# A diagonal state-space loop: chunks read back through a buffer in memory, table products added in PSUM, input factors cut from the state matrices

## The chip, the cores and the metric

The kernel runs on one core of a Trainium2 chip. The metric is the device time of one execution in microseconds (us). Engines are named as the profile names them: PE (matrix products), DVE (vector), ACT (scalar), POOL and SP; each executes its own instructions strictly in the order in which they were written for it, DMA issues included.

## The reference, cut to what matters

A two-layer decoder trunk on 256 tokens of width 1024: attention, a dense feed-forward layer ("ffn"), the state-space layer ("s5") and a layer of eight experts ("moe"). The change is in the state-space layer:

```python
u = (h @ w_in).reshape(B, S, 64, 16)                 # 64 groups of 16 channels
bbr = gr * br - gi * bi;  bbi = gr * bi + gi * br    # input factors, (64, 64 states, 16)
bu_r = einsum('bsgh,gph->sbgp', u, bbr); bu_i = einsum('bsgh,gph->sbgp', u, bbi)
xr, xi = scan over s of  x[s] = a * x[s-1] + bu[s]   # a complex and diagonal, per group and state
y = einsum(xr, c_re) - einsum(xi, c_im) + d_skip * u
z = gelu(y) @ w_glu
out = z[..., :D] * sigmoid(z[..., D:])
```

## The kernel before, in words

The four layers run one after the other, and weights stream from memory on SP's DMA queue through a ring of buffers. In all layers but the experts a weight of 128x1024 is split into a high and a low part, `whi` on ACT (L227) and `wlo` on DVE (L229), three pairs of buffers deep, and each product is made of three matmuls (L253 to L255).

In `s5` the 256 tokens are cut into 32 chunks of 8, and the 64 groups into 8 blocks `b` of 8 groups. First `pu`, the product with `w_in`, is made in two halves of 512 columns; ACT scales each into `ut` (L1040). Then, per block:

- T, `tables` (L865): DVE makes `cp`, the output factors times the powers of `a` (L874), as two products and a sum (L876), and `bt`, the input factors, as two products and a sum (L879, L880). SP loads `bc` and `dd`.
- A, `local` (L885): PE multiplies `bt` by `cp` into `pkk`; ACT copies it to `kk` (L898), DVE adds the skip term (L899), and eight DMAs, four on SP and four on POOL, spread it into the 128x128 blocks of `tt` (L902), which POOL has cleared.
- X, `chunks` (L912): eight DMAs of 32x128 from `ut`, issued on ACT's queue, gather the block's tokens by chunk into `X` (L916).
- U, `chunkT` (L918): PE transposes `X` into `pU`, ACT copies it to `U` (L924).
- S, `states` (L926): PE multiplies `U` by the state matrices `M` into `pS` (L931); DVE rotates (`ri`), scans (`z`), rotates back (`ro`) and writes `W` (L942).
- P, `output` (L945): PE adds `tt`·`U` (L951) and `cp`·`W` (L954) in `py`.
- Z, `gelu` (L957): DVE transposes `py` into `yd`, ACT takes the gelu and the high part `gTh`, DVE the low part `gTl`.
- G and H, `glu`: twelve matmuls into `pz` with one split weight. `pq` is a part of the same product with other columns, for all eight blocks.

The order in which blocks and steps are written is a list, `ORDER`; a scheduler then fixes each engine's own order. Below a block is named by its number: S3 is the state product of block 3. The layer's last loop product is P7. The matrices `M` are made earlier, during the ffn layer, by `s5_tables`: there DVE multiplies the same input matrices by the factors for 8 powers into `mt`, PE transposes them.

Of the kernel before, what the change touches and what calls it, by code (L numbers as in the profile page):

```python
# [10 lines left out]
F32 = mybir.dt.float32  # L11
# [3 lines left out]
AF = mybir.ActivationFunctionType  # L15
ALU = mybir.AluOpType
# [3 lines left out]
P = 128  # L20
D = 1024
KB = D // P
TOK = 256
TB = TOK // P
# [7 lines left out]
CH = 8  # L32
NCK = TOK // CH
# [39 lines left out]
PROL = "0:T0 1:T1 2:A0"  # L73
AQ = "spspspsp"
KBUF = 3
MANUAL = 0
RING, RING2, LOOK = 4, 2, 2
LOOK2 = 3
# [24 lines left out]
class Trunk:  # L103
# [637 lines left out]
    def s5_tables(self, m, t):  # L741
        nc, a, v = self.nc, self.a, self.nc.vector
        G = 64
# [3 lines left out]
        n = lambda nm: t.tile([P, G], F32, tag="z_" + nm, name="z_" + nm)  # L747
# [23 lines left out]
        while k < 8:  # L771
            b = lambda z: z[:, k:k + 1, :].to_broadcast([P, k, G])
# [7 lines left out]
        g = t.tile([P, 2, G], F32, name="gri")  # L780
# [14 lines left out]
            v.tensor_mul(g[:, i, :], u1, den)  # L795
        H = (t.tile([P, 8, G], F32, name="Hr"), t.tile([P, 8, G], F32, name="Hi"))
        gb = [g[:, i:i + 1, :].to_broadcast([P, 8, G]) for i in range(2)]
        self.Bt = m.tile([P, 2, G], F32, name="Bt")
        v.tensor_copy(self.Bt, g)
        yield  # L800
        self.cmul(t, H, (pr[:, 0:8], pi[:, 0:8]), gb, [P, 8, G], "Hc")
        for z in (pr, pi):
# [8 lines left out]
        for i in range(7):  # L811
            q = (t.tile([P, G], F32, tag="rc", name="rc", bufs=2), t.tile([P, G], F32, tag="rs", name="rs", bufs=2))
            self.cmul(t, q, r[-1], r[-1], [P, G], "rq")
            r.append(q)
            if i >= 2:
# [4 lines left out]
                else:  # L820
                    h = max(1, k // 2)
# [8 lines left out]
        for b in range(8):  # L830
            gs = slice(b * 8, b * 8 + 8)
            B = t.tile([P, 2, 8, 16], F32, tag="Bb", name="Bb", bufs=2)
            nc.sync.dma_start(B, a["s5bc"][b][:, 2:4])
            mt = [t.tile([P, 8, 8, 16], F32, tag=f"mt{i}", name=f"mt{i}") for i in range(2)]
            for i in range(2):
                v.tensor_tensor(mt[i], B[:, i, :, None, :].to_broadcast([P, 8, 8, 16]),
                                H[i][:, :, gs].rearrange("p j g -> p g j")[:, :, :, None].to_broadcast([P, 8, 8, 16]), op=ALU.mult)
            v.tensor_tensor(mt[0], mt[0], mt[1], op=ALU.add)
            for q in range(2):
                pt = self.tp((P, 4, P), name="MT")  # L840
                for i in range(4):
                    nc.tensor.transpose(pt[:, i, :], mt[0][:, q * 4 + i].rearrange("p j h -> p (j h)"), self.ident)
                g0 = b % 2 * 8 + q * 4
                nc.scalar.copy(self.M[b // 2][:, g0:g0 + 4, :], pt)
            yield

    def s5(self, h, m, t):
        nc, a, v = self.nc, self.a, self.nc.vector
        mm = nc.tensor.matmul
# [2 lines left out]
        with self.behind((None, self.h_dve, self.t_dve)[H1 // 8 % 4]):  # L852
            self.upto("moe")
        r2 = self.rms(h, "n2", self.t_act if H1 & 32 else None)
        ut = t.tile([P, TB, D], F32, name="ut")
        gh, gl = self.xT("gT")
        CP, T, M8, BT, U, W, Y, XS, DD = {}, {}, {}, {}, {}, {}, {}, {}, {}

        flip = [0]

        def alt(shape, name):
            flip[0] ^= 1
            return (self.gu, self.tp)[flip[0]](shape, name)

        def tables(b):  # L865
            gs = slice(b * 8, b * 8 + 8)
            bc = t.tile([P, 4, 8, 16], F32, tag="bc", name="bc", bufs=2)
            nc.sync.dma_start(bc, a["s5bc"][b])
            DD[b] = t.tile([16, 8, 16], F32, tag="dd", name="dd", bufs=2)
            nc.sync.dma_start(DD[b], a["s5_dd"][:, gs])  # L870
            cp = t.tile([P, 8, 9, 16], F32, tag="cp", name="cp", bufs=KBUF)
            ct = t.tile([P, 8, 9, 16], F32, tag="t16", name="ct", bufs=2)
# [11 lines left out]
            CP[b], M8[b], BT[b] = cp, m8, bt[0]  # L884

        def local(b):
            cp, bt = CP[b], BT.pop(b)
            kk = t.tile([16, 8, P], F32, tag="t16", name="kk", bufs=2)
            tt = T[b] = t.tile([P, 8, P], F32, tag="tt", name="tt", bufs=KBUF)
            nc.gpsimd.memset(tt, 0.0)  # L890
            pk = alt((P, 2, P), name="pkk")
            for q in range(2):
                for i in range(4):
                    g = 2 * i + q
                    mm(pk[32 * i:32 * i + 16, q, :], lhsT=bt[:, g, :], rhs=cp[:, g, 0:8, :].rearrange("p d h -> p (d h)"),
                       start=True, stop=True)
# [14 lines left out]

        def chunks(b):  # L912
            X = XS[b] = self.tmp.tile([NCK, CH, 16, 8], F32, tag="xn", name="X")
            for j in range(CH):
                tb, jj = divmod(j, CH // TB)
                nc.scalar.dma_start(X[:, CH - 1 - j].rearrange("c h g -> c (h g)"), ut[jj * NCK:(jj + 1) * NCK, tb, b * P:(b + 1) * P])  # L916

        def chunkT(b):  # L918
            X = XS.pop(b)
# [25 lines left out]
        def output(b):  # L945
            u, w, cp, tt = U[b], W[b], CP[b], T[b]
            py = Y[b] = alt((P, 2, P), name="py")
            for q in range(2):
                for i in range(4):
                    g = 2 * i + q  # L950
                    mm(py[32 * i:32 * i + 32, q, :], lhsT=u[:, g, :], rhs=tt[:, g, :], start=True, stop=False)  # L951
                for i in range(4):
                    g = 2 * i + q
                    mm(py[32 * i:32 * i + 32, q, :], lhsT=w[:, g, :], rhs=cp[:, g, 1:9, :].rearrange("p d h -> p (d h)"),  # L954
                       start=False, stop=True)

        def gelu(b):  # L957
            py = Y.pop(b)
# [21 lines left out]
        def glu_out(nh):  # L980
            for tb in range(TB):
# [35 lines left out]
        def run(w, k):  # L1017
            if 0 <= k < 8 and (w, k) not in done:
                done.add((w, k))
                steps[w](k)  # L1020
                for e, tag in pf:
                    if e == f"{w}{k}":
                        self.early(tag)

        for n in range(2):
            pu = [self.acc("pu") for _ in range(TB)]
            for u in range(2):
                for hf in range(2):
# [12 lines left out]
            if n == 0:  # L1041
                run("X", 0)
        for i in range(-4, 16):
# [406 lines left out]
def trunk_kernel(ctx: ExitStack, tc: tile.TileContext, a, out, stage=9):  # L1450
    nc = tc.nc
    if MANUAL:
        ctx.enter_context(tc.manual_schedule())
    t = Trunk(ctx, tc, a, out)
    h = t.mla()
    if stage == 1:
        nc.sync.dma_start(out.rearrange("(b p) d -> p b d", p=P), h)
# [117 lines left out]
```

## Time and profile before

| | us |
|---|---|
| median of 3 runs (1354.12 to 1358.92) | 1354.19 |
| the profiled execution | 1351.04 |
| its span, first to last instruction | 1348.9 |
| PE busy in the span | 1271.1 (94%) |
| DVE busy | 500.5 (37%) |
| ACT busy | 315.1 (23%) |
| read from memory | 417.19 MB |

The profiled execution lasted 2.1 us longer than its span. Shares over the whole span hide the layers: attention and ffn fill the first 327 us, `s5` the stretch from there to about 485, the experts the rest. The page's table of 40 slices shows where an engine is busy; a slice is 33.7 us long.

### The profile page before, as it was taken

Reading aid. Unit: us, or ns where it says so; the run is one execution under the profiler, and the core shown is the slowest. Engines: PE = TensorE matmul, PEld = TensorE weight load, DVE = VectorE, ACT = ScalarE, POOL = GpSimd, SP = SyncE. Lnnn points to the kernel's source line nnn. Section 1 sums busy time; section 2 is a strip of 40 time slices with the busy share of each in tenths; the row PEclk is TensorE's granted clock in tenths of the full one; section 3 lists DMA queues with packets and bytes.
Section 4 is the critical chain, followed back from the end, with each engine's and each line's share of the span. In section 5 each row is a group of like instructions: output and inputs, shape, how many; then the busy total and the mean of one; then the engine's idle time right before and its main releaser. Section 6 shows DMA issues by size and latency. Waiting matters only on the chain. (4 is left out here: it accounts for less than half of the span.)

```text
span 1348.9 us, 38996 instructions
## 1 busy us (share of the span) xinstructions
PE 1271.1 (94%) x17345; PEld 882.9 (65%) x17345; DVE 500.5 (37%) x1085; ACT 315.1 (23%) x630; POOL 48.5 (4%) x89
## 2 busy tenths in 40 slices
PE   7898999999888899999999999999999999999973
PEld 6787999997676776666656665555655555665542
DVE  5875989887778750102020011002002002011102
ACT  6764544455323450100010000001000001000001
POOL 3000000001023100000000000000000000000000
PEclk9989999999877899999999999999999999999997
DMA  7303445553444779999999999999999999999993
GB/s 286 125 33 104 178 178 181 195 199 141 159 133 123 258 291 407 416 414 415 416 416 416 418 407 405 417 407 407 415 419 405 405 405 417 413 404 415 408 402 130
DMA packets 80448, 424.26 MB, mean 315 GB/s; under 512 B 14608, under 2 KB 18448, under 8 KB 39824
## 3 DMA queue, kind: packets, MB, share of 16 engines
q1 hardware_dynamic: 76016, 418.79, 78.3%
q0 software_dynamic: 1024, 1.31, 0.7%
q8 instruction: 138, 2.26, 0.7%
q10 hardware_dynamic: 3232, 1.58, 0.5%
q14 instruction: 38, 0.31, 0.1%
HBM read 417.19 MB, written 1.05 MB: 310 GB/s over the span
## 5 line engine op out<-in xcount | busy, mean ns | idle before, releaser
L1235 PE MATMUL pg<-w,xg 128*32 128x256 f32 (+1 forms) x7168 | 492.5, 378 | 5.6 <-DMA w<-in_moe_w 5.5
L1235 PEld LDWEIGHTS pg<-w,xg 128*32 128x32 f32 x7168 | 262.6, 110 | 160.8 <-issue 11.9
L1325 PE MATMUL py<-w,th 128*32 128x256 f32 x4704 | 280.3, 380 | 6.2 <-DMA w<-in_moe_w 6.1
L1271 DVE TENSOR_TENSOR sl<-pg,sl 128x256 f32<-128x256 f32 (+1 forms) x56 | 23.6, 422 | 672.4 <-ACT sl L1270 672.4
L1325 PEld LDWEIGHTS py<-w,th 128*32 128x32 f32 x4704 | 160.4, 110 | 107.0 <-DMA w<-in_moe_w 6.8
L1235 PE MATMUL pu<-w,xg 128*32 128x256 f32 (+1 forms) x2240 | 226.9, 376 | 1.5 <-issue 1.5
L1270 ACT ACTIVATE sl<-pg 128x256 f32<-128x256 f32 (+1 forms) x56 | 21.4, 381 | 653.1 <-PE pg L1235 653.1
L229 DVE TENSOR_TENSOR wlo<-w,whi 128x1024 fp32r<-128x1024 f32 (+1 forms) x120 | 141.3, 1182 | 47.9 <-ACT whi L227 47.6
L227 ACT CAST whi<-w 128x1024 fp32r<-128x1024 f32 (+1 forms) x120 | 121.6, 1019 | 130.2 <-PE pg L254 52.1
L1235 PEld LDWEIGHTS pu<-w,xg 128*32 128x32 f32 x2240 | 100.8, 110 | 48.5 <-issue 2.8
L254 PE MATMUL pg<-n1l,whi 128*128 128x256 f32 x352 | 101.7, 289 | 0.0
L253 PE MATMUL pg<-n1h,whi 128*128 128x256 f32 x352 | 101.4, 288 | 0.1
L255 PE MATMUL pg<-n1h,wlo 128*128 128x256 f32 x352 | 101.5, 289 | 0.0
L253 PEld LDWEIGHTS pg<-n1h,whi 128*128 128x128 f32 x352 | 67.5, 192 | 1.3 <-ACT whi L227 0.3
L254 PEld LDWEIGHTS pg<-n1l,whi 128*128 128x128 f32 x352 | 67.6, 192 | 0.7
L255 PEld LDWEIGHTS pg<-n1h,wlo 128*128 128x128 f32 x352 | 67.4, 192 | 0.0
L253 PE MATMUL fo<-whi,th 128*128 128x512 f32 x88 | 34.6, 394 | 0.3 <-ACT th L700 0.3
L254 PE MATMUL fo<-wlo,th 128*128 128x512 f32 x88 | 34.5, 393 | 0.0
L255 PE MATMUL fo<-whi,tl 128*128 128x512 f32 x88 | 34.3, 390 | 0.0
L1404 POOL TENSOR_TENSOR fx<-h,gF 128x512 f32<-128x512 f32 x1 | 1.3, 1274 | 883.8 <-ACT fjk L1403 883.8
L1273 DVE STREAM_TRANSPOSE th<-sl 128x384 f32<-128x384 f32 (+2 forms) x56 | 29.4, 525 | 2.0
L1369 PE MATMUL psc<-yy,ST 96*128 96x512 f32 (+1 forms) x64 | 24.9, 465 | 5.2 <-ACT yy L1362 2.7
(469 smaller groups left out, 1383.9 us busy)
## 6 DMA issues: line engine op xcount, KB each, us to landing
w<-in_moe_w SPq DMA_DIRECT2D x264, 1024.0 KB, 16.9
w<-in_moe_w SPq DMA_DIRECT2D x144, 512.0 KB, 13.6
w<-in_ffn_gu SPq DMA_DIRECT2D x22, 1024.0 KB, 4.8
w<-in_ffn_dn SPq DMA_DIRECT2D x11, 1024.0 KB, 4.8
w<-in_s_glu SPq DMA_DIRECT2D x8, 1024.0 KB, 6.0
w<-in_mla_o SPq DMA_DIRECT2D x4, 1024.0 KB, 4.8
w<-in_s_in SPq DMA_DIRECT2D x4, 1024.0 KB, 4.7
w<-in_mla_in SPq DMA_DIRECT2D x4, 672.0 KB, 7.4
```

What stands on the lines that cost most here:

```text
L227: nc.scalar.copy(hi[:, :k], w[:, c0:c1])
L229: self.lo_dve = nc.vector.tensor_sub(lo[:, :k], w[:, c0:c1], hi[:, :k].bitcast(F32))
L253: mm(out, lhsT=lh, rhs=rh, start=first, stop=False)
L254: mm(out, lhsT=lh, rhs=rl, start=False, stop=False)
L255: mm(out, lhsT=ll, rhs=rh, start=False, stop=last)
L1235: mm(ps[t // 2][32 * q:32 * q + 32, t % 2, 0:w], lhsT=lhsT, rhs=rhs[:, q], start=first and t % 2 == 0, stop=last and (t % 2 == 1 or t == n ...
L1270: self.silu = nc.scalar.activation(sl[:, ts], src[:, :, 0:k], AF.Silu)
L1271: v.tensor_tensor(sl[:, ts], src[:, :, k:2 * k], sl[:, ts], op=ALU.mult)
L1273: v.transpose(th.rearrange("p t b x -> p (t b x)"), sl.rearrange("p t k -> p (t k)"))
L1325: mm(y[e][b][32 * q:32 * q + 32, i, :], lhsT=th[:, t, fb], rhs=w[:, c * 256:(c + 1) * 256], start=first and i == 0, stop=last and (nt == 2 ...
L1369: mm(ps, lhsT=gath[e][0:CAPS[e], tb * P:(tb + 1) * P], rhs=yy[:, z], start=z == 0, stop=z == 1)
L1404: (nc.gpsimd, v)[n if XM else 1].tensor_mul(x[:, 1, s], h[:, 1, s], gF[:, s])
```

## The change

- X is one DMA on SP instead of eight on ACT. `ut` is now a buffer of one half, written by two DMAs on ACT's queue to a buffer in memory (`du0`, `du1`), and `X` is read back from there with the chunks reversed by the access pattern.
- The sum of the two products of `cp` is gone: both stay as tiles, and PE multiplies by each and adds in PSUM, in `pkk` and in `py`.
- `bt` is gone: the factors for power 0 are copied by ACT from `mt` to `BT` in the ffn layer, and `bc` loads half as much.
- `kk` has one buffer of its own (it shared two with a product of `cp`), `tt` two buffers instead of three, and `ut` takes turns with `X` in the two buffers `xn`.

```diff
 def s5_tables
-        self.Bt = m.tile([P, 2, G], F32, name="Bt")
-        v.tensor_copy(self.Bt, g)
+        self.BT = m.tile([P, G, 16], F32, name="BT")
...
             v.tensor_tensor(mt[0], mt[0], mt[1], op=ALU.add)
+            nc.scalar.copy(self.BT[:, gs, :], mt[0][:, :, 0, :])
 def s5
-        ut = t.tile([P, TB, D], F32, name="ut")
+        UT = [self.dram.tile([TB, P, 512], F32, name=f"du{n}") for n in range(2)]
 def tables
-            bc = t.tile([P, 4, 8, 16], F32, tag="bc", name="bc", bufs=2)
+            bc = t.tile([P, 2, 8, 16], F32, tag="bc", name="bc", bufs=2)
...
-            for i, (o, z) in enumerate(((cp, self.pr), (ct, self.pi))):
-                v.tensor_tensor(o, bc[:, i, :, None, :].to_broadcast([P, 8, 9, 16]),
+            for i, z in enumerate((self.pr, self.pi)):
+                v.tensor_tensor(CP[b][i], bc[:, i, :, None, :].to_broadcast([P, 8, 9, 16]),
...
-            v.tensor_tensor(cp, cp, ct, op=ALU.add)
-            bt = [t.tile([P, 8, 16], F32, tag=f"bt{i}", name=f"bt{i}") for i in range(2)]
-            for i in range(2):
-                v.tensor_tensor(bt[i], bc[:, 2 + i], self.Bt[:, i, gs, None].to_broadcast([P, 8, 16]), op=ALU.mult)
-            v.tensor_tensor(bt[0], bt[0], bt[1], op=ALU.add)
 def local
-            kk = t.tile([16, 8, P], F32, tag="t16", name="kk", bufs=2)
-            tt = T[b] = t.tile([P, 8, P], F32, tag="tt", name="tt", bufs=KBUF)
+            kk = t.tile([16, 8, P], F32, tag="kk", name="kk", bufs=1)
+            tt = T[b] = t.tile([P, 8, P], F32, tag="tt", name="tt", bufs=2)
...
-                    mm(pk[32 * i:32 * i + 16, q, :], lhsT=bt[:, g, :], rhs=cp[:, g, 0:8, :]...,
-                       start=True, stop=True)
+                for n in range(2):
...
+                        mm(pk[32 * i:32 * i + 16, q, :], lhsT=self.BT[:, b * 8 + g, :], rhs=cp[n][:, g, 0:8, :]...,
+                           start=n == 0, stop=n == 1)
 def chunks
-            for j in range(CH):
-                tb, jj = divmod(j, CH // TB)
-                nc.scalar.dma_start(X[:, CH - 1 - j]..., ut[jj * NCK:(jj + 1) * NCK, tb, b * P:(b + 1) * P])
+            n, i = divmod(b, 4)
+            row = UT[n][:, :, :]
+            src = bass.AP(tensor=row.tensor, offset=row.offset + i * P, ap=[[512, NCK], [NCK * 512, CH], [1, P]])
+            nc.sync.dma_start(X.rearrange("c j h g -> c j (h g)")[:, ::-1], src)
 def output
-                    mm(py[32 * i:32 * i + 32, q, :], lhsT=w[:, g, :], rhs=cp[:, g, 1:9, :]..., start=False, stop=True)
+                for n in range(2):
...
+                        mm(py[32 * i:32 * i + 32, q, :], lhsT=w[:, g, :], rhs=cp[n][:, g, 1:9, :]..., start=False, stop=n == 1)
 in s5, after each half of pu
+            ut = self.tmp.tile([P, TB, 512], F32, tag="xn", name="ut")
             for tb in range(TB):
-                nc.scalar.activation(ut[:, tb, n * 512:(n + 1) * 512], pu[tb], AF.Copy, scale=r2[:, tb:tb + 1])
+                nc.scalar.activation(ut[:, tb], pu[tb], AF.Copy, scale=r2[:, tb:tb + 1])
+                nc.scalar.dma_start(UT[n][tb], ut[:, tb])
```

ACT's order from the end of the first half of `pu` on, before:

```order
L1040 ACTIVATE ut<-pu,n2y 128x512
L916 DMA X<-ut 32x128
L1040 ACTIVATE ut<-pu,n2y 128x512
L916 DMA X<-ut 32x128 x7
L227 CAST whi<-w 128x1024 x2
L898 COPY kk<-pkk 16x256 x4
L227 CAST whi<-w 128x1024
L924 COPY U<-pU 128x256
L916 DMA X<-ut 32x128
```

and now (the product of `local` for block 0 has moved ahead of it, into the first half of `pu`):

```order
L1039 ACTIVATE ut<-pu,n2y 128x512
L1040 DMA du_3871<-ut 128x512
L1039 ACTIVATE ut<-pu,n2y 128x512
L228 CAST whi<-w 128x1024
L1040 DMA du_3871<-ut 128x512
L228 CAST whi<-w 128x1024 x3
L1039 ACTIVATE ut<-pu,n2y 128x512
L1040 DMA du_3872<-ut 128x512
L1039 ACTIVATE ut<-pu,n2y 128x512
L921 COPY U<-pU 128x256
L1040 DMA du_3872<-ut 128x512
```

Seven gathers stood between `ut` and the next `whi`; now no more than one write stands between any two. SP's order at the blocks 0 to 2, now (before, the same queue without its `X` rows):

```order
L898 DMA tt<-kk 16x8x16
L898 DMA tt<-kk 16x8x48
L898 DMA tt<-kk 16x8x80
L898 DMA tt<-kk 16x8x112
L913 DMA X<-du_3871 32x8x128
L871 DMA dd<-in_s_dd 16x128
L869 DMA bc<-in_s5bc 128x256
L206 DMA w<-in_s_glu 128x2048
L913 DMA X<-du_3871 32x8x128
L206 DMA w<-in_s_glu 128x2048
L898 DMA tt<-kk 16x8x16
```

The reads stand among the copies of `tt` and the weights, each behind what precedes it. DVE's order around `W` of block 2, before:

```order
L229 TENSOR_TENSOR wlo<-w,whi 128x1024
L937 SCALAR_TENSOR_TENSOR z<-m8b,ri_4315 128x256
L964 TENSOR_TENSOR gTl<-yd,gTh 128x256
L907 TENSOR_TENSOR ro_4323<-z,E 128x256
L908 TENSOR_TENSOR ro_4324<-z,F 64x256
L909 TENSOR_TENSOR ro_4324<-z,F 64x256
L907 TENSOR_TENSOR ri_4446<-pS,E 128x256
L942 TENSOR_TENSOR W<-ro_4323,ro_4324 128x8x31
```

and now:

```order
L874 TENSOR_TENSOR cp<-bc,pi 128x1152
L934 SCALAR_TENSOR_TENSOR z<-m8b,ri_4319 128x256
L230 TENSOR_TENSOR wlo<-w,whi 128x1024
L903 TENSOR_TENSOR ro_4327<-z,E 128x256
L904 TENSOR_TENSOR ro_4328<-z,F 64x256
L905 TENSOR_TENSOR ro_4328<-z,F 64x256
L230 TENSOR_TENSOR wlo<-w,whi 128x1024
L939 TENSOR_TENSOR W<-ro_4327,ro_4328 128x8x31
```

The split of the weight after next has moved ahead of `W`.

## Rows read from the trace of the kernel before

**Rows 1.** The page's 40 slices: busy tenths of PE and the clock granted to it, in tenths.
```profile
PE   7898999999888899999999999999999999999973
PEclk9989999999877899999999999999999999999997
```

**Rows 2.** Busy time by stretch (us from the span's start, its length; then PE, PEld, DVE, ACT, POOL with their instructions, the granted clock, DMA share, GB/s): the loop of the eight blocks, what follows it up to the experts, the experts.
```profile
347.00:457.00 110.00, 89.56 (x724) 72.23 (x722) 80.51 (x145) 35.76 (x71) 27.09 (x55) 0.75 0.47 127
457.00:500.00 43.00, 42.51 (x225) 33.04 (x217) 30.46 (x80) 26.78 (x48) 0.00 (x0) 1.00 0.82 327
600.00:1330.00 730.00, 715.32 (x12417) 422.02 (x12408) 89.92 (x192) 51.65 (x137) 0.00 (x0) 1.00 1.00 407
```

**Rows 3.** Waits of PE in the loop, 347 to 457 us: who waited for whom, us in total, times, the longest.
```profile
PE pS L931 <- ACT U L924: 7.5, 5, 2.9
PE pz L253 <- ACT gTh L963: 3.9, 1, 3.9
PE pU L922 <- DMA dd<-in_s_dd: 3.3, 2, 2.1
PE pU L922 <- DMA X<-ut: 2.0, 2, 1.7
PE pkk L895 <- ACT kk L898: 1.6, 1, 1.6
```

**Rows 4.** Groups of ACT in the same stretch: count, busy us, mean ns of one, idle just before them and what ended it.
```profile
L227 ACT CAST whi<-w 128x1024 fp32r<-128x1024 f32 x12 | 12.5, 1046 | 31.7 <-PE pz L255 18.7 <-DMA X<-ut 9.5 <-PE pu L255 3.2
L898 ACT COPY kk<-pkk 16x256 f32<-16x256 f32 x32 | 11.6, 363 | 10.0 <-DMA dd<-in_s_dd 5.6 <-DMA X<-ut 4.1
L924 ACT COPY U<-pU 128x256 f32<-128x256 f32 x8 | 3.0, 370 | 10.4 <-DMA X<-ut 8.3 <-PE pU L922 1.7 <-PE py L951 0.4
L962 ACT ACTIVATE yd<-yd 128x256 f32<-128x256 f32 x7 | 2.9, 417 | 12.8 <-DVE yd L960 12.8
L963 ACT CAST gTh<-yd 128x256 fp32r<-128x256 f32 x7 | 2.8, 406 | 0.3
...
L962 ACT ACT_TABLE_LOAD x1 | 1.3, 1283 | 7.2 <-DMA X<-ut 7.2
```

**Rows 5.** The gathers by source line: issues on ACT's queue, ns of one issue (min, median, max), first and last start.
```profile
L916 ACTq DMA_DIRECT2D X<-ut x64: 513/601/1882, 347.8 to 416.7; - x64
```

**Rows 6.** ACT in order of time (start, us, instruction, idle before it and who ended it), at the second half of `pu`.
```profile
347.08 0.69 ACT L1040 ACTIVATE ut<-pu,n2y 128x512 f32<-128x512 f32 x1 [0.94 <-PE pu L255]
...
348.49 6.31 ACTq L916 DMA_DIRECT2D X<-ut  x7
354.84 1.99 ACT L227 CAST whi<-w 128x1024 fp32r<-128x1024 f32 x2 [5.68 <-DMA X<-ut]
```

**Rows 7.** PE in order of time, same columns: the stop in the second half of `pu`; S0; a `pkk` group at the high and one at the low clock; S2; the first and last of a block's twelve `pz` matmuls at the low clock and at the high; the last `py` group of P7.
```profile
352.77 0.39 PE L255 MATMUL pu<-whi,n2l 128*128 128x512 f32 x1
...
355.94 1.22 PE L253 MATMUL pu<-whi,n2h 128*128 128x512 f32 x2 [2.22 <-ACT whi L227]
...
365.36 1.87 PE L931 MATMUL pS<-U,M 128*128 128x32 f32 x16
367.16 0.63 PE L895 MATMUL pkk<-cp,bt 128*16 128x128 f32 x16
...
376.63 1.08 PE L895 MATMUL pkk<-cp,bt 128*16 128x128 f32 x16
...
380.51 3.62 PE L931 MATMUL pS<-U,M 128*128 128x32 f32 x16 [1.42 <-ACT U L924]
...
408.74 0.80 PE L253 MATMUL pz<-whi,gTh 128*128 128x512 f32 x1
...
413.60 0.53 PE L255 MATMUL pz<-whi,gTl 128*128 128x512 f32 x1
...
453.24 0.39 PE L253 MATMUL pz<-whi,gTh 128*128 128x512 f32 x1
...
455.75 0.39 PE L255 MATMUL pz<-whi,gTl 128*128 128x512 f32 x1
...
456.75 0.40 PE L954 MATMUL py<-cp,W 128*32 128x128 f32 x8
```

**Rows 8.** DVE: in order of time, the `W` that answers to S0; then groups of the loop, 347 to 457 us (count, busy us, mean ns, idle before).
```profile
371.86 0.40 DVE L942 TENSOR_TENSOR W<-ro,ro 128x248 f32<-128x248 f32 x1
...
L229 DVE TENSOR_TENSOR wlo<-w,whi 128x1024 fp32r<-128x1024 f32 x12 | 14.5, 1212 | 8.8 <-ACT whi L227 8.8
L876 DVE TENSOR_TENSOR cp<-cp,ct 128x1152 f32<-128x1152 f32 x7 | 9.4, 1348 | 0.0
L879 DVE TENSOR_TENSOR bt<-bc,Bt 128x128 f32<-128x128 f32 x13 | 3.6, 281 | 0.0
...
L960 DVE STREAM_TRANSPOSE yd<-py 128x256 f32<-128x256 f32 x7 | 3.1, 441 | 2.3 <-PE py L954 2.3
```

**Rows 9.** DMA issues by line in 347 to 457 and at the kernel's end (KB each, median us from issue to landing): a load, and the kernel's output, which goes to memory; then the smallest, median and largest landing of the gathers and of the output.
```profile
bc<-in_s5bc SPq DMA_DIRECT2D x8, 256.0 KB, 3.3
out<-fx ACTq DMA_DIRECT2D x2, 256.0 KB, 5.7
...
DMA to landing us min/median/max: 1.7/2.7/6.6
...
DMA to landing us min/median/max: 3.1/4.8/6.7
```

More of the change, by code (lines that the diff above doesn't have):

```diff
@@ L75 @@
 KBUF = 3
+KQ = "sss"
 MANUAL = 0
@@ L854, in s5 @@
         r2 = self.rms(h, "n2", self.t_act if H1 & 32 else None)
-        ut = t.tile([P, TB, D], F32, name="ut")
+        UT = [self.dram.tile([TB, P, 512], F32, name=f"du{n}") for n in range(2)]
         gh, gl = self.xT("gT")
-        CP, T, M8, BT, U, W, Y, XS, DD = {}, {}, {}, {}, {}, {}, {}, {}, {}
+        CP, T, M8, U, W, Y, XS, DD = {}, {}, {}, {}, {}, {}, {}, {}
         flip = [0]
@@ L866, in tables @@
             gs = slice(b * 8, b * 8 + 8)
-            bc = t.tile([P, 4, 8, 16], F32, tag="bc", name="bc", bufs=2)
-            nc.sync.dma_start(bc, a["s5bc"][b])
+            bc = t.tile([P, 2, 8, 16], F32, tag="bc", name="bc", bufs=2)
+            nc.sync.dma_start(bc, a["s5bc"][b][:, 0:2])
             DD[b] = t.tile([16, 8, 16], F32, tag="dd", name="dd", bufs=2)
             nc.sync.dma_start(DD[b], a["s5_dd"][:, gs])
-            cp = t.tile([P, 8, 9, 16], F32, tag="cp", name="cp", bufs=KBUF)
-            ct = t.tile([P, 8, 9, 16], F32, tag="t16", name="ct", bufs=2)
-            for i, (o, z) in enumerate(((cp, self.pr), (ct, self.pi))):
-                v.tensor_tensor(o, bc[:, i, :, None, :].to_broadcast([P, 8, 9, 16]),
+            CP[b] = [t.tile([P, 8, 9, 16], F32, tag=f"cp{i}", name="cp", bufs=KBUF) for i in range(2)]
+            for i, z in enumerate((self.pr, self.pi)):
+                v.tensor_tensor(CP[b][i], bc[:, i, :, None, :].to_broadcast([P, 8, 9, 16]),
                                 z[:, :, gs].rearrange("p j g -> p g j")[:, :, :, None].to_broadcast([P, 8, 9, 16]), op=ALU.mult)
-            v.tensor_tensor(cp, cp, ct, op=ALU.add)
-            bt = [t.tile([P, 8, 16], F32, tag=f"bt{i}", name=f"bt{i}") for i in range(2)]
-            for i in range(2):
-                v.tensor_tensor(bt[i], bc[:, 2 + i], self.Bt[:, i, gs, None].to_broadcast([P, 8, 16]), op=ALU.mult)
-            v.tensor_tensor(bt[0], bt[0], bt[1], op=ALU.add)
             m8 = t.tile([P, 8, NCK], F32, tag="m8b", name="m8b", bufs=2)
@@ L883, in tables @@
             nc.gpsimd.memset(m8[:, :, 0:1], 0.0)
-            CP[b], M8[b], BT[b] = cp, m8, bt[0]
+            M8[b] = m8
         def local(b):
-            cp, bt = CP[b], BT.pop(b)
-            kk = t.tile([16, 8, P], F32, tag="t16", name="kk", bufs=2)
-            tt = T[b] = t.tile([P, 8, P], F32, tag="tt", name="tt", bufs=KBUF)
+            cp = CP[b]
+            kk = t.tile([16, 8, P], F32, tag="kk", name="kk", bufs=1)
+            tt = T[b] = t.tile([P, 8, P], F32, tag="tt", name="tt", bufs=2)
             nc.gpsimd.memset(tt, 0.0)
@@ L892, in local @@
             for q in range(2):
-                for i in range(4):
-                    g = 2 * i + q
-                    mm(pk[32 * i:32 * i + 16, q, :], lhsT=bt[:, g, :], rhs=cp[:, g, 0:8, :].rearrange("p d h -> p (d h)"),
-                       start=True, stop=True)
+                for n in range(2):
+                    for i in range(4):
+                        g = 2 * i + q
+                        mm(pk[32 * i:32 * i + 16, q, :], lhsT=self.BT[:, b * 8 + g, :], rhs=cp[n][:, g, 0:8, :].rearrange("p d h -> p (d h)"),
+                           start=n == 0, stop=n == 1)
             for i in range(4):
@@ L951, in output @@
                     mm(py[32 * i:32 * i + 32, q, :], lhsT=u[:, g, :], rhs=tt[:, g, :], start=True, stop=False)
[L952 to L955, printed above, removed]
+                for n in range(2):
+                    for i in range(4):
+                        g = 2 * i + q
+                        mm(py[32 * i:32 * i + 32, q, :], lhsT=w[:, g, :], rhs=cp[n][:, g, 1:9, :].rearrange("p d h -> p (d h)"),
+                           start=False, stop=n == 1)
         def gelu(b):
@@ L1454, in trunk_kernel @@
     t = Trunk(ctx, tc, a, out)
+    t.dram = ctx.enter_context(tc.tile_pool(name="dram", bufs=1, space=bass.MemoryType.DRAM))
     h = t.mla()
```

1 line of the change is left out of this document (removed).

## Prediction

> **What bounds the kernel now.** I read the page's slices first, to find where PE stands still. From slice 15 on PE is busy nine tenths and more at the full clock [rows 1], and in the experts the DMA engines' share is 1.00 [rows 2]: that part runs at the pace of its weights and simply starts when `s5` lets it. From 457 to 500 us PE is busy 42.5 of 43.0 us at a clock of 1.00 [rows 2]. The weak place is slices 10 to 13, the loop of the eight blocks. There PE is busy 89.6 of 110 us at a mean granted clock of 0.75, and no engine is full: DVE 80.5, ACT 35.8 [rows 2]. So the loop is bound by who waits for whom, and a microsecond won before 457 is a microsecond of the whole, since what follows is unchanged.
>
> PE's waits in the loop are next [rows 3]: 7.5 us for `U` on ACT, 5.3 for `X` (3.3 of it put down to `dd`, which PE does not read at a transpose; it landed last), 3.9 for `gTh`, 1.6 for `kk`, and 2.2 for `whi` at one stop [rows 7]. That is 20.5 us, all of the 20.4 that PE stands. ACT's groups say why ACT is late: 9.5 us of idle time ahead of `whi`, 8.3 ahead of `U`, 7.2 ahead of the table load, 4.1 ahead of `kk`, each ended by a gather `X` [rows 4]. Nobody waits there for data. ACT is issuing: 64 gathers of 0.60 us each are 38.5 us of ACT's line [rows 5], in which nothing else of ACT starts. The clearest case stands at 348.5: seven issues, 6.3 us, and only then the two `whi` [rows 6], while PE stops at 353 and resumes at 355.9 [rows 7].
>
> **The change, part by part.**
>
> *ACT.* The 64 issues go. Four writes come; at the gathers' 0.60 us that is 2.4 us.
>
> *The way of the data.* Instead of ACT to `X` it is now ACT, a write to memory, a read. No row shows a read that waits for a write. The nearest write is the kernel's output, 256 KB as here: 5.7 us on ACT's queue, 3.1 to 6.7 over all [rows 9]. For the read of 128 KB the nearest is `bc`, 256 KB in the same stretch, 3.3; the gathers took 1.7 to 6.6 [rows 9]. I take 5.7 and 3.3. This matters at block 0, where nothing hides it, and for the others only if a read is issued less than 3.3 us before its transposes. The Trainium skill, in "DMA: Bandwidth & Descriptors", section "Anatomy of one DMA", says that most of the fixed 2 us of a transfer is the receipt of its last write, longest when the target is memory, and fits 2.0 us plus the bytes at 436 GB/s (on GpSimd's path); by that the write would take an estimated 2.6 us, the output's rows say more, and the sum below would be about 1 us shorter.
>
> *DVE.* The sum of `cp` goes, 1.35 us a block, and three small operations of `bt` of 0.28 [rows 8]: 2.2 us a block, 9.4 + 3.6 us and the sums of `bt` in this stretch, some 15 of its 80.5. It shortens DVE's line, not PE's.
>
> *PE.* `pkk` is made twice: one more group, 0.63 us at the high clock and 1.08 at the low [rows 7]. `py` has six groups instead of four; one group takes 0.22 us from start to start at the high clock (0.40 busy in the row [rows 7]), and at the low clock, by the ratio of `pkk`, 0.38. Together 1.1 to 1.8 us a block, 9 to 15 us in all. This falls on the engine that is waited for, and is hidden only where PE would stand.
>
> *The ffn layer.* Eight copies into `BT`, each smaller than a `gTh` of 0.41 us [rows 4], so under 3.3 us of ACT. PE is eight to nine tenths busy there [rows 1], and ACT waits for it; I cost them at nothing, 3.3 us if that cover were gone. Buffers: `kk` alternated with a product of `cp` before and so had one already; `tt` with two waits for the P of two blocks before, which is long done. Both at nothing.
>
> **The sum**, from the orders now built, with the durations of the rows. Prices between the clocks: `pkk` doubled 1.6 us, a `py` 1.7, a block's `pz` 3.7 (2.9 at the high clock, 5.4 at the low [rows 7]), `pU` 1.05, S 1.9 (3.6 at the low clock [rows 7]). Three chains recur. E, from a `py` to the next `pz`: `yd`, gelu, `gTh`, 0.44 + 0.42 + 0.41 = 1.3 us [rows 4, 8]. W, from the end of S to `W`: 367.2 to 372.3, 5.0 us [rows 7, 8]. V, new, where DVE's order puts `wlo` ahead of `W`: end of `pz`, `whi` 1.05, `wlo` 1.21, `W` 0.40, 2.7 us [rows 4, 8].
>
> 1. The second half of `pu` loses its stop and its low clock. 24 of its 48 products remain at 352.8; at 0.23 us they end at 358.3. The second write is issued at 350.1 (behind `ut` and one `whi`), lands at 355.8, the read at 359.1. `pU` and `pkk` of blocks 0 and 1 follow: S0 at 361.8, where it is at 365.4 now [rows 7]. 3.6 us won.
> 2. S1 ends at 368.3, `W` of block 0 is at 369.1, P0 ends at 370.4, then yd behind block 1's scan, the table load of 1.3 and E: `pz` 0 at 374.
> 3. Half of `pz` 0, P1, `pU`, `U`: S2 at 379.1, now 380.5 [rows 7]; but P1 and half of `pz` 0, which come after it now, are done.
> 4. S2, `pkk`, the rest of `pz` 0, `pz` 1: 387.6. Chain V, 2.7 us of standing PE; P2 and `pU`: 393; S3 to 395.
> 5. `pkk`, `pU`, `pz` 2, S4, P3: 405. DVE reaches `yd` of block 3 only behind the next `wlo`: `pz` 3 at 408.4, 3.4 us of standing.
> 6. `pz` 3, `pkk`, P4, `pU`, `U`: S5 at 417.
> 7. S5, `pkk`, `pU`, S6, `pz` 4, P5: 428.8. E. `pz` 5, `pkk`, P6: 437.1. E. `pz` 6, `pU`, S7: 444.5.
> 8. Chain W, 5.0 us beside products of `pq`, and the rest of P7, 1.4: 450.9. P7 ends at 457.15 now [rows 7].
>
> So 6.2 us are won: 3.6 of them before S0, and in the loop some 13 us of standing PE remain and the added products eat most of what ACT and DVE give. The profiled execution took 1351.04 us (span 1348.9), and becomes 1344.8. The median of the runs, 1354.19, lies 3.15 above it; I add that: **1348.0 us**. A measurement of this kernel can tell about 0.5%, 6.8 us, from no change, so the forecast stands right at that bound.
>
> **The rivals.**
>
> *PE stays at the full clock.* The granted clock is 1.00 where PE does not stop (457 to 500) and 0.75 in the loop [rows 2]. If the missing stops keep it up, `pz` falls to 2.9, `pkk` to 1.25, `py` to 1.3: 1.6 us a block, over seven blocks 11 more, so 17 us won: 1337. For it: the stops behind ACT's issues go. Against it: steps 2, 4 and 5 still stop for 3 us each.
>
> *No relief.* ACT's issues only fill time in which ACT would wait for PE (18.7 us) and DVE (12.8) anyway [rows 4]; the stops come back as those waits, the 9 to 15 us of added products cancel the 3.6 and DVE's 15: 1354, within 4. Against it are the 29 us of idle time that ended with an issue [rows 4]. The Trainium skill, same page, section "Issuing engines are not separate DMA queues", holds that all issuers share the DMA engines, so that moving an issue saves only the sequencer's time, usually small beside the transfer; by it this rival is the likely one. Here the issuing alone is 38.5 us [rows 5], which speaks against the "small".
>
> *Slower: the reads on SP's line.* SP too executes in order. A read stands behind four copies of `tt`, which wait for `kk`, and behind a buffer that the transposes two blocks back must free. In my walk the reads lead their transposes by 0.7 us (block 1), 3 (block 5) and 5 and more. If reads land at the gathers' worst, 6.6 us [rows 9], or SP is held up that long, each block waits out a whole read: 8 x 3.3 = 26.4, less the 5.3 that PE waits for `X` already [rows 3], less the 6.2: 15 us longer, 1369. It decides at a lead under 3.3 us in most blocks.
>
> **How the numbers follow.** The walk 0.45, with its own range of 1342 to 1354, since each price has two ends; the full clock 0.22; no relief 0.18; slower 0.15. The range, 1336 to 1360, takes in the first three and the write's and read's upper ends (1.0 and 3.3 us at block 0); most of the fourth is left out. Faster by more than 0.5%: the full clock whole, half of the walk, a little of "no relief": 0.47. Slower: most of the fourth: 0.14. Between: 0.39.
>
> **What would show it.** Right: no stop of PE in the second half of `pu`; S0 near 362; ACT's idle time ended by `X` gone, and instead "`whi` for `pz`" and "gelu for `yd`" as its largest waits; PE waiting for `gTh` and `W` where it waited for `U`; writes landing in about 5.7 us, reads in about 3.3; P7 ending at 451. The full clock would show as a clock of 0.85 or more in the loop. Wrong: PE waiting for `X` for more than 10 us in total, SP's `tt` or weights waiting for reads, or a gain that is lost again between 457 and 500, as when the last weights of the product come late because they now stand behind block 7's copies on SP.

## The result, and the profile after

The changed kernel takes 1360.47 us (median of 20 runs, 1355.43 to 1366.64), the kernel before 1353.85 on the same chips (20 runs): the ratio is 1.0055, 95% interval 1.004 to 1.007. It is slower by half a per cent where I had forecast 1348.0. The profiled execution took 1359.44 us, its span is 1357.6 (before: 1348.9).

The slices, then the stretches of [rows 2] (columns as there), of the changed kernel:

```profile
PE   6988999999989899999999999999999999999974
...
PEclk9999999999966999999999999999999999999997
```

```profile
347.00:457.00 110.00, 96.33 (x896) 77.32 (x895) 65.87 (x112) 34.14 (x67) 26.85 (x56) 0.78 0.44 115
457.00:500.00 43.00, 41.71 (x244) 31.34 (x242) 32.23 (x86) 23.14 (x40) 0.00 (x0) 1.00 0.86 348
600.00:1330.00 730.00, 713.82 (x12460) 423.77 (x12452) 88.56 (x189) 50.33 (x134) 0.00 (x0) 1.00 1.01 411
```

Against [rows 2], DVE fell by 14.6 us, as forecast, and PE is busy 6.8 us more in the same 110. P7 ends at 462.31 (before at 457.15). The waits of PE (columns as in [rows 3]) and of ACT in the loop:

```profile
PE pz L254 <- ACT gTh L961: 8.8, 4, 3.1
PE py L952 <- DVE W L939: 5.2, 3, 2.5
PE py L948 <- DMA tt<-kk: 0.7, 1, 0.7
```

```profile
ACT whi L228 <- PE pz L256: 21.1, 4, 8.5
ACT U L921 <- PE pU L919: 19.3, 7, 5.3
ACT yd L960 <- DVE yd L958: 12.6, 5, 8.1
ACT L960 <- DVE yd L958: 7.2, 1, 7.2
ACT kk L894 <- DMA tt<-kk: 4.8, 1, 4.8
```

All waits for `U` and `X` are gone from PE, and ACT's large waits now end with PE or DVE, none with an issue; one of 4.8 us ends when the copies out of the single `kk` have landed. PE stands 14.7 us, not 20.5. The new transfers, the issue of a read (columns as in [rows 5]) and the landings of reads and writes, are short:

```profile
L913 SPq DMA_DIRECT2D X<-du x8: 572/580/1056, 354.9 to 444.1; - x8
...
DMA to landing us min/median/max: 2.6/3.2/6.2
```

```profile
L1040 ACTq DMA_DIRECT2D du<-ut x4: 326/331/357, 349.2 to 361.2; - x4
...
DMA to landing us min/median/max: 2.5/2.9/4.4
```

Of the 8.7 us between the two spans, 1.4 lie before the first `ut` (348.50 for 347.08; in the profiles of all kernels here it lies between 347.1 and 351.8), 3.7 in the loop, some 0.3 up to the first product of the experts, and 3.1 in the experts (820.3 us from the first `pg` to the last, before 817.2). One profile each can't tell whether the last belongs to the change: in the other kernels here it was 814.1 to 820.2. The runs below were made on several chips, each beside the kernel before, so times of different rounds are compared by the ratios in the table (0.01 is 13.5 us). They compare loops too: from the start of the first `ut` to the end of P7, where PE's busy and standing time add up to the length.

| kernel | loop us | PE busy | stands | clock | last read of X issued | ratio to before (95%) |
|---|---|---|---|---|---|---|
| before | 110.1 | 89.6 | 20.4 | 0.75 | - | 1 |
| changed | 113.8 | 99.0 | 14.8 | 0.79 | 444.1 | 1.0055 (1.004 to 1.007) |
| e1 | 106.0 | 91.4 | 14.7 | 0.76 | 427.2 | 1.0005 (0.999 to 1.0019) |
| e2 | 112.4 | 95.2 | 17.2 | 0.74 | 432.6 | 1.002 (1.0007 to 1.0033) |
| e3 | 117.1 | 95.5 | 21.6 | 0.72 | | not comparable |
| e4 | 112.1 | 96.2 | 15.9 | 0.82 | - | 1.0007 (0.9986 to 1.0029) |
| e5 | 118.2 | 98.7 | 19.5 | 0.71 | 450.0 | 1.0056 (1.0034 to 1.0078) |
| e9 | 106.2 | 92.0 | 14.2 | 0.86 | 426.5 | 0.9981 (0.9968 to 0.9995) |
| e10 | 120.1 | 102.3 | 17.8 | 0.77 | 436.0 | 1.0045 (1.0031 to 1.0059) |
| e11 | 101.6 | 89.6 | 12.0 | 0.88 | 406.2 | 0.9955 (0.9939 to 0.9971) |
| e12 | 113.5 | 92.2 | 21.3 | 0.76 | 444.0 | 1.0059 (1.0043 to 1.0076) |
| e13 | 115.5 | 93.6 | 21.9 | 0.78 | - | 1.0046 (1.0028 to 1.0064) |
| e14 | 103.2 | 92.5 | 10.7 | 0.85 | 405.0 | 0.997 (0.9955 to 0.9985) |
| e15 | 111.8 | 92.8 | 19.1 | 0.76 | 434.6 | 1.0046 (1.0028 to 1.0065) |
| e16 | 106.6 | 94.4 | 12.2 | 0.82 | 412.5 (ACT) | 0.9954 (0.9936 to 0.9971) |
| e17 | 115.3 | 94.1 | 21.3 | 0.84 | 408.4 | 0.9989 (0.9976 to 1.0003) |
| e18 | 130.8 | 103.5 | 27.4 | 0.70 | - | 1.0129 (1.0113 to 1.0145) |

(The three runs of a fixed order, e6 to e8, do part of `pz` after P7, so their loops are not set beside these. Each loop here is from one profile, and those of e9 to e11 and e13 to e18 hold six more products of `pq`, some 2 us, than those of the kernel before and of the changed kernel.)

### The profile page after: what moved, and what is told of

It reads as the page before. It is cut to its first block, busy times and chain, and to the rows that moved or that the text cites. A ratio compares the mean times of both kernels' runs of the same rounds, so it can differ in the third digit from the quotient of the medians.

```text
span 1357.6 us, 39435 instructions
## 1 busy us (share of the span) xinstructions
PE 1282.5 (94%) x17601; PEld 890.3 (66%) x17601; DVE 486.4 (36%) x1052; ACT 317.5 (23%) x638; POOL 48.3 (4%) x89
## 5 line engine op out<-in xcount | busy, mean ns | idle before, releaser
L1270 ACT ACTIVATE sl<-pg 128x256 f32<-128x256 f32 (+1 forms) x56 | 21.4, 382 | 655.8 <-PE pg L1235 655.8
L254 PE MATMUL pg<-n1h,whi 128*128 128x256 f32 x352 | 101.6, 289 | 0.4 <-ACT whi L228 0.3
```

Of the source, the lines that this page charges most:

```text
L254: mm(out, lhsT=lh, rhs=rh, start=first, stop=False)
L1270: self.silu = nc.scalar.activation(sl[:, ts], src[:, :, 0:k], AF.Silu)
```

## The experiments

**First round: is it PE's products, or the way over memory?** Theory A was my first: the loop is PE's work plus its standing, and the added products ate the relief.

e1, tables summed by DVE again, with the buffers of before; the rest as changed:
```diff
+            v.tensor_tensor(cp, cp, ct, op=ALU.add)
...
-            kk = t.tile([16, 8, P], F32, tag="kk", name="kk", bufs=1)
-            tt = T[b] = t.tile([P, 8, P], F32, tag="tt", name="tt", bufs=2)
+            kk = t.tile([16, 8, P], F32, tag="t16", name="kk", bufs=2)
+            tt = T[b] = t.tile([P, 8, P], F32, tag="tt", name="tt", bufs=KBUF)
...
-                for n in range(2):
-                    for i in range(4):
+                for i in range(4):
```


> The changed kernel with the table products summed by DVE again, as before (and with the buffers of before for cp, kk and tt); chunks over memory and input factors from the state matrices stay. Theory A, PE's ledger: the length of the loop is PE's busy time plus its standing; the second products are 10.8 us of PE work in the loop (pkk 6.3 to 11.5, py 10.2 to 16.2), the standing that went is only 5.8 (20.5 to 14.7). Without the products the loop is 5 to 11 us shorter than in the changed kernel, if standing does not come back: 1349 to 1355 where the changed kernel has 1360.5. Theory B, the way over memory (reads on SP's line, writes on ACT's) costs the time: it stays at 1358 or more. Theory C, only the order that was built anew costs it: anything, but PE's busy time in the loop then does not explain it.

Measured: 1352.57 us, 106.0 in the loop. The way over memory alone does not make it slow; where its reads stand in SP's line comes back in the third round.

e2, the same with `bt` from `bc` as before, so that only the way of the chunks is changed:
```diff
-            bc = t.tile([P, 2, 8, 16], F32, tag="bc", name="bc", bufs=2)
+            bc = t.tile([P, 4, 8, 16], F32, tag="bc", name="bc", bufs=2)
...
+            v.tensor_tensor(bt[0], bt[0], bt[1], op=ALU.add)
```


> The kernel before with the chunks alone formed over memory (one read per block on SP, writes on ACT's queue); sums of the tables and the input factors as before. Theory A: PE's work is that of before (89.8 us in the loop), ACT loses 64 issues, so the 20.5 us of standing can only shrink: 1343 to 1353 where before has 1353.9. Theory B: slower than before, 1356 or more, with PE waiting for X or tt. Beside the other run without the second products it prices the input factors: up to 2 us.

1355.40 us, between the ranges of theories A and B. The 64 issues are off ACT's line, and nothing is won: 17.2 us of standing remain. The input factors are worth 2 to 3 us (e1 against e2), the orders differing.

e3, the changed kernel without the second products of `pkk` and `py`:
```diff
-                for n in range(2):
+                for n in (0,):
```


> The changed kernel with the second product of each pair left out in pkk and py, so that part of each table is missing from the result; the second table is still built by DVE. All else, DVE and the transfers too, is that of the changed kernel. Theory A: PE busy in the loop falls from 100.6 to about 90 us; if the standing stays at 14.7 us the loop is 11 us shorter (1349.5), if half of the freed time becomes standing, 5 us (1355). Theory B: no change, 1358 to 1362.

Its result changes what the router reads; the experts make twice the `pg` products (14464 for 7168) and the kernel takes 2248.9 us, so only the loop counts. The loop became longer, 117.1 us, with two fifths of the `pkk` and `py` products gone:
```profile
349.00:466.10 117.10, 95.45 (x708) 76.27 (x706) 68.12 (x117) 33.36 (x66) 27.97 (x56) 0.72 0.49 139
```
Busy time fell by 3.5 us only, at a clock of 0.72 for 0.79 (the eight S alone took 23.8 us for 21.4), and PE stands 6.8 us more. So theory A's sum does not hold by itself; the orders of PE, DVE and ACT are not quite those of the changed kernel, and this is no price of the products.

e4, the kernel before with these products made twice:
```diff
+                for n in range(2):
-                       start=True, stop=True)
+                           start=n == 0, stop=n == 1)
```


> The kernel before with each product of cp in pkk and py made twice, from the same summed table, so that these products count double in the result; nothing else is changed. It prices the added products alone. Theory A: PE's busy time in the loop grows from 89.8 by 10 to 11 us; hidden is only what falls into the 20.5 us of standing: 1357 to 1365. Theory B: the 20.5 us of standing swallow them: 1353 to 1356.

1353.10 us. `pkk` and `py` took 10.4 us more of PE, but the loop only 2.0: 4.5 went into the standing, and the clock rose from 0.75 to 0.82, at which S took 17.5 us for 20.5.

**Second round: buffers, or the order?** From here "theory B" means the buffers, and theory O that the time lies in the order on each engine, which the scheduler builds anew for every kernel.

e5, e1 with the changed kernel's buffers (the two lines of `kk` and `tt` above taken back: `tt` two, `kk` one of its own):


> The first experiment (chunks over memory, input factors from the state matrices, tables summed by DVE) with the buffers of the changed kernel: tt two instead of three, kk one of its own instead of a place in turn with ct. After the first four runs the ledger alone has fallen: without the second products, but with the buffers and a newly built order, the loop (from the first ut to the end of P7) took 117.1 us, the changed kernel 113.9, the first experiment 106.0. Theory B, the buffers: 1358 or more, with tt waiting for P and PE waiting for tt. Theory O, the order that the scheduler builds anew: nothing of the kind, 1350 to 1355, or any other value with PE's largest waits elsewhere than at tt and kk.

1360.70 us, as slow as the changed kernel without its products.

e6, e7 and e8: the blocks issued in the order of the program on every engine, in the kernel before, the changed kernel, and e5:
```diff
+        with self.tc.manual_schedule():
             for i in range(-4, 16):
```


> The kernel before with the eight blocks issued in the order of the program (ORDER) on every engine, not in the order that the scheduler finds. It is the base of the next two, which have the same order of PE's products. In this order W of a block and the pz between stand at fixed places. Theory O: the loop's length changes by several us one way or the other through order alone: 1340 to 1370.

> The changed kernel with the same fixed order. Theory O: what cost 3.7 us in the loop was the order; at equal order the changed kernel is faster than the fixed kernel before, by what ACT and DVE give less what the products cost: 2 to 10 us faster. Theory A (PE's products): slower than the fixed kernel before by 2 to 8 us, with PE's busy time up by 10 or 11.

> The run with the two-buffer tt (chunks over memory, factors from the state matrices, tables summed by DVE) with the same fixed order. Against the run before it, it prices the second products at fixed order and buffers: theory A 8 to 11 us less than the changed kernel at this order, theory O 0 to 4 less. Against the fixed kernel before it prices the way of the chunks and the factors: faster by 2 to 10, since 64 issues leave ACT's line.

1368.53 (ratio 1.0108, 1.0073 to 1.0144), 1360.16 (1.0057, 1.0037 to 1.0076) and 1365.87 (1.0097, 1.0064 to 1.013). At one order of PE the change is faster than before by 8 us, and with its products it is 6 us faster than with DVE's sums. All three are slow orders, and PE waits in e7, then in e8:
```profile
PE pU L919 <- DMA X<-du: 19.3, 5, 6.0
```
```profile
PE pU L920 <- DMA X<-du: 29.2, 7, 8.4
```
Here PE is seen waiting for the reads. As e8 waits 9.9 us more for `X`, the 6 us are no price of PE's products alone.

e9, the changed kernel with one 8 KB load moved:
```diff
 def tables(b):
-            DD[b] = t.tile([16, 8, 16], F32, tag="dd", name="dd", bufs=2)
-            nc.sync.dma_start(DD[b], a["s5_dd"][:, gs])
 def local(b):
+            DD[b] = t.tile([16, 8, 16], F32, tag="dd", name="dd", bufs=1)
+            nc.sync.dma_start(DD[b], a["s5_dd"][:, b * 8:b * 8 + 8])
```


> The changed kernel with one small load moved: dd (8 KB) is loaded with a block's local step, into one buffer, not an iteration earlier with its tables into two. No work is added or taken away; but the scheduler then builds another order on PE, in which S7 stands ahead of P6 instead of behind it, and S3, S4 and S6 stand further ahead of their P as well. Theory O (the order that the scheduler builds costs the time, not the products, the way over memory, nor the wait for a buffer): 1349 to 1356 where the changed kernel has 1360.5. Theory B (two buffers of tt) and theory A (PE's products): 1359 to 1362, as the changed kernel.

1349.26 us. The same work, 10 us less by the ratios: the work as such does not cost it. The edit changes the place of a small load and, with it, the order that the scheduler builds. PE between 370 and 440 us, the changed kernel and then e9:
```profile
370.00:440.00 70.00, 61.41 (x548) 49.09 (x552) 43.21 (x80) 18.32 (x40) 16.09 (x36) 0.66 0.32 80
```
```profile
370.00:440.00 70.00, 60.47 (x668) 48.61 (x663) 50.23 (x92) 21.71 (x46) 19.84 (x42) 0.81 0.46 116
```
In about as much busy time e9 makes 120 matmuls more, at a clock of 0.81 and not 0.66. PE in order of time in the changed kernel:
```profile
392.24 0.43 PE L948 MATMUL py<-tt,U 128*32 128x128 f32 x8
395.12 0.60 PE L952 MATMUL py<-cp,W 128*32 128x128 f32 x10 [2.46 <-DVE W L939]
...
397.87 3.62 PE L928 MATMUL pS<-U,M 128*128 128x32 f32 x16
...
418.35 0.80 PE L254 MATMUL pz<-whi,gTh 128*128 128x512 f32 x1 [3.11 <-ACT gTh L961]
```
and in e9:
```profile
390.08 1.93 PE L928 MATMUL pS<-U,M 128*128 128x32 f32 x16
393.31 0.66 PE L948 MATMUL py<-tt,U 128*32 128x128 f32 x8 [0.28 <-DMA tt<-kk]
```
S3 stands ahead of P2 in e9 and fills the time in which the changed kernel stands for W; there S3 comes behind, at the low clock (3.62 us for 1.93).

e10, e11: the read of the chunks ahead of the local step in the loop's order; e11 also with three buffers of `tt` and `dd` as in e9:
```diff
-ORDER = "S0 Z1 T-2 A-1 G2 U-1 X-2 P0 H2"
+ORDER = "S0 Z1 T-2 X-2 A-1 G2 U-1 P0 H2"
```


> The changed kernel with the read of the chunks ahead of the local step in the loop's order (S0 Z1 T-2 X-2 A-1 G2 U-1 P0 H2), so that on SP it is not behind the copies of tt. Work and buffers are those of the changed kernel; the order that results has S of a block ahead of P of the one before all through the loop. Theory O: 1345 to 1355. Theories A and B: 1359 to 1362.

> The run before it with three buffers for tt as in the kernel before (dd loaded with the local step, to make room). Theory B: faster than with two by 4 or more. Theory O: within 3 us of it. If the products cost nothing beside that, this is the version that may beat both kernels: 1343 to 1352.

1359.19, a miss: S of each block stands ahead of P of the one before, and the loop is still 120.1 us long. So that place of S is not enough. The edit also did not do on SP what it was made for: the read of block 7 goes out at 435.98, again behind four copies of `tt` (431.73). 1346.61 for e11, faster than both kernels.

e12, e5 with three buffers of `tt`:
```diff
-            tt = T[b] = t.tile([P, 8, P], F32, tag="tt", name="tt", bufs=2)
+            tt = T[b] = t.tile([P, 8, P], F32, tag="tt", name="tt", bufs=KBUF)
```


> The run with a two-buffer tt (1360.7) with three buffers for tt and kk still with one of its own. Its order on PE is the same as that run's, row for row by tile, and not the first experiment's (1352.6), which has three and lets kk take turns with ct. Theory B, the wait for a buffer of tt: 1351 to 1354. Theory O: 1358 to 1362, since the order stays.

1360.10: the third buffer of `tt` does not help, so theory B is out for `tt`. Between e1 and e12 the edit is that of `kk` alone, and no row of ACT's or PE's waits shows a wait for its buffer in e12; that the order it brings costs the time is what remains, and is not tested apart.

**Third round: is it the change's own, and why?** e13 moves `dd` in the kernel before (the diff of e9); e14 is e11 with two buffers of `tt`; e15 is e14 with the tables summed by DVE (the diff of e1, its buffers too).
```diff
-            tt = T[b] = t.tile([P, 8, P], F32, tag="tt", name="tt", bufs=KBUF)
+            tt = T[b] = t.tile([P, 8, P], F32, tag="tt", name="tt", bufs=2)
```

> The kernel before with dd loaded with a block's local step into one buffer, as in the run of that edit on the changed kernel (1349.3 instead of 1360.5). The order that the scheduler then builds for PE has S of each block ahead of the pz and P of the one before, to the end. If the gain of that edit is a better order and no part of the change, the kernel before gains too: 1342 to 1350. If dd's load was in the way only of the changed kernel's reads on SP: 1352 to 1355.

> The fastest run so far (1346.6: the read ahead of the local step, dd loaded with it, three buffers of tt) with two buffers of tt, as the changed kernel has. The order on PE, DVE, ACT and SP is the same row for row; only POOL sets tt to zero at other places. Theory O: 1345 to 1349. Theory B: 1351 or more.

> The chunks over memory and the factors from the state matrices, tables summed by DVE, with the read ahead of the local step and dd loaded with it: an order that also has S ahead throughout. Against the run before it, it prices the second products where the order stands well. Theory A, products on a busy PE: 5 to 11 us less, 1337 to 1342. If the clock gives back what the products take: within 3 us of it.

1356.93, 1346.85, 1356.77. The kernel before wins nothing by the edit, it loses 5 us, more than either forecast. e14 equals e11: two buffers do. e15 missed both its ranges: with DVE's sums the kernel is 10 us slower than e14, not faster. PE is busy as long in both, 92.5 us in e14 for 92.8, at a clock of 0.85 for 0.76, and stands 8.4 us less in e14. This is no price of the products: e15's order is another, with the read of block 7 issued 30 us later, and the clock, DVE's 9 us of sums and the order are not separated.

Up to here one number went with the time in all runs with a read on SP and a scheduled order: when the read of block 7 is issued (table; with the loop's length it goes less well). SP in the changed kernel:
```profile
416.11 2.53 SPq L898 DMA_DIRECT2D tt<-kk  x4
418.68 1.05 SPq L913 DMA_DIRECT2D X<-du  x1
...
440.05 3.36 SPq L898 DMA_DIRECT2D tt<-kk  x4
443.45 0.59 SPq L206 DMA_DIRECT2D w<-in_s_glu  x1
444.09 0.86 SPq L913 DMA_DIRECT2D X<-du  x1
```
```profile
SPq L898 <- DVE kk L895: 53.0, 7, 13.1
```
Each of these reads goes out behind four copies of `tt`, and the copies wait 53.0 us in all for `kk`. S7 follows only at 454.62, behind P6. Theory R: this place in SP's line sets the order. It is the first round's theory B in a narrower form: not the way over memory, but the line in which its reads stand.

e16 takes the reads off SP, e17 the copies, e18 the copies in the kernel before:
```diff
-            nc.sync.dma_start(X.rearrange("c j h g -> c j (h g)")[:, ::-1], src)
+            nc.scalar.dma_start(X.rearrange("c j h g -> c j (h g)")[:, ::-1], src)
```
```diff
-AQ = "spspspsp"
+AQ = "pppppppp"
```


> The changed kernel with the eight reads of the chunks issued by ACT instead of SP; all else, buffers and dd too, is as in the changed kernel. Over the runs so far the time goes with the moment at which SP issues the read of block 7: 405 us in the two fastest (1346.6, 1346.9), 426 and 427 in those at 1349.3 and 1352.6, 435 and 436 at 1356.8 and 1359.2, 444 to 450 in the changed kernel and the two others at 1360. Theory R: in SP's line the reads stand behind the copies of tt, which wait for kk, and the scheduler, which keeps every queue in order, puts U and S of the blocks behind them. Off SP's line the reads go early and S stands a block ahead: 1345 to 1351. Against it: if the moment is only a mark of a slow loop, it stays at 1358 to 1362.

> The changed kernel with the reads on SP as they are, but all eight copies of tt of a block on POOL's queue instead of four there and four on SP's. The other way to free the reads. Theory R: 1345 to 1351, if eight copies in a row on POOL do not hold up tt; if they do, PE waits for tt, up to 1 us a block, and it is 1351 to 1357. Against theory R: 1358 to 1362.

> The kernel before with all copies of tt on POOL's queue: the control to the run before it. Its gathers are on ACT's queue, so no read stands behind copies on SP. Theory R: within 4 us of the kernel before, 1349 to 1357. If the copies on SP hold up something else that both kernels have (the weights), it gains as much as the changed kernel does: 1343 to 1348.

1345.30, 1350.58 and 1369.41 us. e16 changes nothing in the program but the queue of eight reads, and the changed kernel becomes 14 us faster by the ratios, the fastest here with e11. From the first `ut` to the first product of the experts its profile shows 148.5 us, the changed kernel's 157.4. The read of block 7 goes out 32 us earlier:
```profile
L913 ACTq DMA_DIRECT2D X<-du x8: 567/568/960, 357.0 to 412.5; - x8
```
e17 is 9 us faster by the ratios, but its profile does not bear theory R out. The read goes out early, at 408.4, and yet the loop is 115.3 us long, and from the first `ut` to the first product of the experts it takes 157.2 us, as the changed kernel does; PE now waits for `tt`:
```profile
PE py L948 <- DMA tt<-kk: 7.9, 4, 3.7
```
Of the 6.9 us between the spans of these two profiles, 5.3 lie in the experts (815.0 us) and 1.4 ahead of the first `ut`. The experts' weights stand on SP too: their fourth to sixth load goes out at 442 to 448 us in e17, in the changed kernel at 457 to 460. So the copies may cost through the weights as well as through the reads; no run separates the two. The control, which has no reads on SP, was forecast within 4 us of before and loses 18; why so much I did not follow, and it shows how far an order can move the time by itself. What is shown: the same work with its reads on another queue (e16) or a small load elsewhere (e9) is 10 to 14 us faster. That the reads' place in SP's line is the reason rests on e16, on the table up to e15 and on the waits for `X` in e7 and e8; that e16 merely met a better order is not excluded, since the scheduler's choices leave no row.

## Why the prediction was wrong, point by point

*Step 1* held in its mechanism: no stop in the second half of `pu`. That S0 came at 361.94 (forecast 361.8) is partly luck: in the forecast it waits for the write and the read, in the trace for `pu`, which ended at 360.0 and not at 358.3 (the first `ut` was 1.4 us later), and the `pkk` ahead of it took 1.07 us, not 1.6. The write landed in 2.9 us where I took 5.7 from the kernel's output [rows 9]; the read in 3.2, forecast 3.3. The Trainium skill, "DMA: Bandwidth & Descriptors", section "Anatomy of one DMA", would give the write an estimated 2.6 by its fit for GpSimd's path. For these writes that was nearer than the output's row.

*Steps 3 to 7 failed, by the "prices between the clocks" of S and `pz`.* `pz` 0 began at 375.27 (374), S2 at 382.37 (379.1), S3 ended at 401.5 (395), `pz` 3 began at 418.35 (408.4), P7 ended at 462.3 (450.9). The standing was nearly right, 14.8 us for 13, and so were the added products: `pkk` and `py` grew from 6.3 + 10.2 to 11.5 + 16.2, 11.2 us in the range of 9 to 15. The prices of the products as a whole were not:

| product | forecast us each | measured busy / count |
|---|---|---|
| S | 1.9 | 21.4 / 8 = 2.68 |
| `pz` of a block | 3.7 | 31.1 / 7 = 4.45 |
| `py` | 1.7 | 16.2 / 8 = 2.03 |
| `pkk` | 1.6 | 11.5 / 7 = 1.65 |

That is 8 x 0.78 + 7 x 0.75 + 8 x 0.33 + 7 x 0.05 = 14.5 us too little; these busy times overlap by 4.3 us, and with 1.8 of standing it makes 12, the miss of 11.4. Most of it lay in products that the change does not touch, and the kernel before, by the same count of its trace, had 20.5 us for eight S (2.57 each) and 29.5 for seven `pz` (4.22). I had set `pz` by eye between a row at either clock, and S at its price at the high one [rows 7]. One addition would have caught it: 89.6 busy, less the 1.4 of low clock that step 1 takes from `pu`, 9 to 15 added and 13 of standing are 110 to 116 us, no less than the 110 of before. The forecast of a gain contradicted its own terms.

*"ACT."* The issues went, as said, but ACT waits for PE and DVE instead. That is what the rival *no relief* said, and e2, which moves the chunks alone, has 1.002. But e2's reads stand on SP too, block 7's at 432.6, so it does not tell a relief of no use from one that late reads took back. The Trainium skill, same page, "Issuing engines are not separate DMA queues", has only the sequencer's time saved by issuing elsewhere, usually little; the outcome of e2 agrees, though the 38.5 us of issuing [rows 5] were not small.

*The slower rival* probably had the right place, SP's line, and the wrong sign to look for. In the changed kernel no wait of PE names `X`, the reads landed in 3.2, and I had it decide at "a lead under 3.3 us". Its sign is there only where the order is fixed (e7, e8). In the changed kernel, by theory R, the order had been built around the late reads, so the transposes were late as well, and the cost shows as waits for W and `gTh` and as a clock of 0.66. The same eight transfers from another queue are worth 1% (e16).

*Buffers "at nothing"*: right for `tt` (e12, e14). For `kk` PE waits nothing and ACT once 4.8 us, but with its own buffer comes an order that is 7 to 8 us slower (e5 and e12 against e1).

*PE at the full clock*: not in the changed kernel (0.79), but e9, e11 and e14 show 0.85 to 0.88; the fastest of them is at 1346.6, not 1337.

The parts of the change do not make the kernel slower in themselves: in e14 and e16 with all of them, and in e11 with three buffers of `tt`, it beats the kernel before by 0.3 to 0.5% and itself as given by 1%. Whether another order would help the kernel before as much is open; the three tried (e6, e13, e18) made it slower.

## What to carry to other kernels

Before walking an order step by step, add up the bounding engine: its busy time, what is added, what standing you leave; and take prices of unchanged work from the groups' sums, not from single rows. Where a scheduler builds the order, a result is that of one order: move a small thing that does no work (a load's place, a queue) and see how far the time moves, before blaming the work that was added; then see in the profile in which stretch it moved. A transfer placed in a queue behind others that wait is late even if, as in the changed kernel, no engine is seen waiting for it.

## What the runs showed of the hardware

Added products seem to pay for themselves in part: with 10.4 us more of `pkk` and `py` in e4 the mean granted clock of the loop was 0.82 instead of 0.75, and the unchanged S 3 us cheaper; with products taken away in e3 the clock was 0.72 instead of 0.79, and S 2.4 us dearer. Both kernels' orders differ a little from their originals, so that this is a tendency and not a price.
